# Holding back the first four output stores of a sparse convolution and issuing them from ScalarE's queue

## The chip, the cores and the metric

One core of one Trainium2 chip. The metric is device time of one execution in microseconds (us). The profile's span (first to last instruction) is about 2 us shorter. A transfer is "issued" when an engine's queue starts it and "landed" when its last byte is reported written. In the profile lines PE is TensorE, DVE VectorE, ACT ScalarE, POOL GpSimd and SP SyncE; a q behind the name (ACTq) is that engine's instruction queue, and PEclk is the clock granted to TensorE in tenths of full speed. A run on one core is called slow when it is over 1.5% above the fastest of the same kernel; fast runs alone enter the ratios.

## The reference

A 3x3 convolution, padding 1, 16 images of 64 channels of 64x64, 128 output channels. The weights are 90% zeros, but scattered, so the kernel treats them as dense.

```python
batch, c_in, h, w, c_out, k = 16, 64, 64, 64, 128, 3
x_pad = np.pad(x, ((0, 0), (0, 0), (pad, pad), (pad, pad)), mode='constant')
output[b, co] += weight[co, ci, kh, kw] * x_pad[b, ci, kh:kh+h, kw:kw+w]   # for all b, co, ci, kh, kw
```

In bytes: 16.8 MB of input and 33.6 MB of output, both fp32.

## The kernel before

Two images (64 channels each) stand one above the other on 128 partitions, so the work is eight pairs. All input loads but the first half pair (fp32, on SyncE's queue) are queued at the start on GpSimd's queue and cast to bf16 on the way. Each pair has four blocks of 16 rows. A block, but for the very first, is three products on TensorE (a shared one, even rows, odd rows); ScalarE copies the shared product to SBUF and VectorE adds it to the other two, into an output tile of 2 MB per image. Seven such tiles are taken in turn; the first also serves as landing place of the first half pair of input.

```python
o_pool = ctx.enter_context(tc.tile_pool(name="o", bufs=7))
psum_pool = ctx.enter_context(
    tc.tile_pool(name="psum", bufs=8, space=bass.MemoryType.PSUM)
)
# ...
x_head = o_pool.tile([128, H, W], FP32, name="o")
# ...
for p in range(1, NP):
    nc.gpsimd.dma_start(out=xs[p], in_=pair(p))
# ...
    shared = product([(s, G1, 0, 1)], 8)              # in twos(): one block
    for n in range(2):
        c = p_pool.tile([128, 8, W], FP32, name="pc")
        nc.scalar.copy(out=c, in_=shared[n])          # L161
    # ...
            nc.vector.tensor_tensor(                  # L168
                out=o[n][:, first : r0 + 16 : 2, :], in0=ps[n], in1=pc[n], op=ADD
            )
# ...
for p in range(NP):
    o = [o_pool.tile([C_OUT, H, W], FP32, name="o") for _ in range(2)]
    # ... four blocks; the last pair is stored in halves
    if not last:
        for n in range(2):
            nc.sync.dma_start(out=out[2 * p + n], in_=o[n])
```

Of the kernel before, what the change touches and what calls it, by code (L numbers as in the profile page):

```python
# [27 lines left out]
def kernel(  # L28
# [6 lines left out]
    nc = tc.nc  # L35

    B, C_IN, H, W = x.shape
# [106 lines left out]
    def direct(p, o, r0, rows):  # L144
        ps = product(
            [(xs[p], G1, r0, 1), (xs[p], G0, r0 - 1, 1), (xs[p], G2, r0 + 1, 1)], rows
        )
        nc.scalar.copy(out=o[0][:, r0 : r0 + rows, :], in_=ps[0])  # L148
        nc.vector.tensor_copy(out=o[1][:, r0 : r0 + rows, :], in_=ps[1])  # L149

    def twos(p, o, r0):
        t0 = r0 // 2
        s = s_pool.tile([128, 8, W], BF16, name="s")
        nc.gpsimd.tensor_tensor(  # L154
            out=s, in0=xs[p][:, r0 : r0 + 16 : 2, :], in1=xs[p][:, r0 + 1 : r0 + 16 : 2, :], op=ADD
        )
        shared = product([(s, G1, 0, 1)], 8)
        pc = []
# [3 lines that stand above are left out]
            pc.append(c)  # L162
        even = [(xs[p], G21, r0 + 1, 2), (xs[p], G0, r0 - 1, 2)]
        odd = [(xs[p], G01, r0, 2), (xs[p], G2, r0 + 2, 2)]
        for first, terms in ((r0, even), (r0 + 1, odd)):
            ps = product(terms, 8)
            for n in range(2):
                nc.vector.tensor_tensor(  # L168
                    out=o[n][:, first : r0 + 16 : 2, :], in0=ps[n], in1=pc[n], op=ADD
                )  # L170

    for p in range(NP):
        o = [o_pool.tile([C_OUT, H, W], FP32, name="o") for _ in range(2)]
        last = p == NP - 1
        for blk in range(4):
            r0 = 16 * blk
            if BLOCKS[p][blk] == "T":
                twos(p, o, r0)
            else:
                for r, rows in ((r0, 8), (r0 + 8, 8)):  # L180
                    direct(p, o, r, rows)
            if last and blk % 2 == 1:
                for n in range(2):
                    rows = slice(r0 - 16, r0 + 16)
                    nc.sync.dma_start(out=out[2 * p + n][:, rows, :], in_=o[n][:, rows, :])
        if not last:
            for n in range(2):
                nc.sync.dma_start(out=out[2 * p + n], in_=o[n])


# [28 lines left out]
```

## Time and profile before

| | before |
|---|---|
| time, median (first 3 runs) | 127.66 us (127.59 to 127.90) |
| span of the profile | 125.4 us |
| TensorE's products | 7.1 to 109.2 us without a gap |
| last two stores issued, landed | 111.2 and 111.8, 121.8 and 124.2 us |
| DMA | full from about 1.8 to 122 us |

The strips cut the span in 40 slices of 3.1 us; a digit is the busy share in tenths. The lines themselves, and how they are read, stand in the prediction below.

### The profile page before, as it was taken

The page shows a single profiled execution, that of the slowest core. Times are in us where ns is not written, and L with a number is a line of the kernel's source. Part 1 is how long each engine was busy: PE and PEld are TensorE (multiplying, and loading weights), DVE is VectorE, ACT ScalarE, POOL GpSimd, SP SyncE. Part 2 cuts the span into 40 slices and gives each one's busy share as a digit, 9 for nine tenths or more (in the row PEclk, how much of TensorE's full clock was granted, in tenths as well). Part 3 has the DMA queues.
Part 4 walks back from the last instruction along what each step waited for, and adds up shares of the span by engine and source line. Part 5 has one row for each costly group of instructions (what it writes and reads, how often), then busy time and mean ns, then how long its engine had stood idle before and what let it go on. Part 6 is the DMA issues. An engine that isn't in the chain of part 4 may idle for free.

```text
span 125.4 us, 2486 instructions
## 1 busy us (share of the span) xinstructions
PE 107.5 (86%) x1002; PEld 58.8 (47%) x1002; DVE 82.4 (66%) x135; ACT 39.0 (31%) x71; POOL 40.7 (32%) x45
## 2 busy tenths in 40 slices
PE   6679999999999999999999999999999999920000
PEld 6435555555555555555555555555555555500000
DVE  0463877877787778777877787778777877760000
ACT  4555323333333333333333333333333333300000
POOL 6936533333333333333333333333333300000000
PEclk9999999999999999999999999999999999997555
DMA  5999999989999999999999999999999999999980
GB/s 146 338 222 220 212 214 220 191 259 350 324 311 337 308 293 319 342 316 308 426 429 423 408 429 434 450 416 434 418 418 429 429 444 423 434 397 423 423 369 10
DMA packets 4044, 42.93 MB, mean 342 GB/s; under 512 B 448, under 2 KB 448, under 8 KB 704
## 3 DMA queue, kind: packets, MB, share of 16 engines
q1 hardware_dynamic: 2880, 34.90, 66.2%
q0 software_dynamic: 1152, 7.86, 30.7%
q8 instruction: 8, 0.13, 0.4%
q14 instruction: 4, 0.03, 0.1%
HBM read 17.07 MB, written 33.55 MB: 404 GB/s over the span
## 4 chain that ended last, share of the span: by engine, by line
PE 81%; DMA 4%; DVE 1%; issue 1%; DVEq 0%; SPq 0%
PE ps L135 81%; DMA o<-in_x_dram 4%; DVE o L168 1%; DVEq L214 0%; DVE x L87 0%; SPq L60 0%; DVEq L168 0%
## 5 line engine op out<-in xcount | busy, mean ns | idle before, releaser
L168 DVE TENSOR_TENSOR o<-ps,pc 128x512 f32<-128x512 f32 x124 | 77.8, 686 | 22.1 <-PE ps L135 19.8
L135 PE MATMUL ps<-x,wT 64*128 64x504 bf16 (+3 forms) x780 | 88.8, 373 | 1.5 <-DVE x L87 1.5
L135 PEld LDWEIGHTS <-wT 64*128 64x128 bf16 x966 | 55.2, 94 | 49.4 <-issue 1.5
L154 POOL TENSOR_TENSOR s<-x 128x512 bf16<-128x512 bf16 x31 | 35.6, 1152 | 57.7 <-PE ps L135 41.5
L161 ACT COPY pc<-ps 128x512 f32<-128x512 f32 x62 | 33.3, 589 | 64.0 <-issue 61.8
L135 PE MATMUL ps<-s,wT 64*128 64x512 bf16 (+1 forms) x186 | 25.7, 377 | 0.0
L74 PE MATMUL ps<-idle_rhs 128*128 128x128 bf16 x27 | 3.1, 310 | 1.0 <-DVE idle_rhs L71 1.0
L67 POOL DMA_DIRECT2D x<-in_x_dram x7 | 3.7, 561 | 0.0
L74 PEld LDWEIGHTS <-idle_rhs 128*128 128x128 bf16 x27 | 2.8, 144 | 1.0 <-DVE idle_rhs L71 1.0
L91 DVE CAST w_bf<-w_sb 128x192 bf16<-128x192 f32 (+1 forms) x4 | 1.3, 382 | 3.0 <-DMA w_sb<-in_weight_dram 3.0
L149 DVE COPY o<-ps 128x512 f32<-128x512 f32 x2 | 1.4, 692 | 2.0 <-PE ps L135 2.0
L148 ACT COPY o<-ps 128x512 f32<-128x512 f32 x2 | 1.2, 586 | 2.4 <-PE ps L135 2.4
L87 ACT CAST x<-o 128x576 bf16<-128x576 f32 (+1 forms) x2 | 1.5, 802 | 0.5 <-DMA o<-in_x_dram 0.5
L91 ACT ACT_TABLE_LOAD x1 | 1.3, 1283 | 0.7 <-PEq L203 0.7
L97 PE MATMUL ps<-ident,w_bf 128*128 128x128 bf16 x9 | 1.1, 292 | 0.4 <-DVE w_bf L91 0.4
L87 DVE CAST x<-o 128x576 bf16<-128x576 f32 x1 | 0.5, 460 | 1.4 <-DMA o<-in_x_dram 1.4
L91 ACT CAST w_bf<-w_sb 128x64 bf16<-128x64 f32 (+1 forms) x2 | 0.7, 418 | 1.9 <-DMA w_sb<-in_weight_dram 1.9
L97 PEld LDWEIGHTS <-w_bf 128*128 128x128 bf16 x9 | 0.8, 128 | 0.8 <-DVE w_bf L91 0.8
L101 DVE TENSOR_TENSOR wT<-ps,wT 128x384 bf16<-128x384 f32 x2 | 1.0, 550 | 0.0
L63 POOL DMA_DIRECT2D x<-in_x_dram x1 | 0.7, 696 | 0.8 <-POOLq L203 0.8
L71 DVE MEMSET idle_rhs<- 128x64 uint32 x1 | 0.1, 112 | 0.8 <-PEq L203 0.8
L110 ACT CAST wT<-ps 128x384 bf16<-128x384 f32 x1 | 0.5, 481 | 0.4 <-PE ps L97 0.4
(8 smaller groups left out, 1.9 us busy)
## 6 DMA issues: line engine op xcount, KB each, us to landing
out_dram<-o SPq DMA_DIRECT2D x14, 2048.0 KB, 19.8
x<-in_x_dram POOLq DMA_DIRECT2D x7, 1024.0 KB, 29.3
out_dram<-o SPq DMA_DIRECT2D x4, 1024.0 KB, 12.3
o<-in_x_dram SPq DMA_DIRECT2D x1, 1024.0 KB, 5.4
x<-in_x_dram POOLq DMA_DIRECT2D x1, 512.0 KB, 7.5
w_sb<-in_weight_dram SPq DMA_DIRECT2D x1, 288.0 KB, 3.1
```

The source lines that it names most:

```text
L67: nc.gpsimd.dma_start(out=xs[p], in_=pair(p))
L74: nc.tensor.matmul(idle_ps, idle_rhs, idle_rhs, start=True, stop=True)
L87: copy(out=xs[0][:, a:b, :], in_=x_head[:, a:b, :])
L91: copy(out=w_bf4[:, g, a:b, :], in_=w_v[:, k : k + b - a, :])
L97: nc.tensor.matmul(wps[:, j, :], src, ident, start=True, stop=True)
L101: nc.vector.tensor_tensor(out=wT[:, g], in0=wps, in1=wT[:, G1], op=SUB)
L135: nc.tensor.matmul(ps[n][:, lo:hi, c_lo:c_hi], tap(g, kw, n), src[q, a:b:step, c_lo + kw - 1 : c_hi + kw - 1], start=(i == 0), stop=(i == ...
L148: nc.scalar.copy(out=o[0][:, r0 : r0 + rows, :], in_=ps[0])
L149: nc.vector.tensor_copy(out=o[1][:, r0 : r0 + rows, :], in_=ps[1])
L154: nc.gpsimd.tensor_tensor(out=s, in0=xs[p][:, r0 : r0 + 16 : 2, :], in1=xs[p][:, r0 + 1 : r0 + 16 : 2, :], op=ADD)
L161: nc.scalar.copy(out=c, in_=shared[n])
L168: nc.vector.tensor_tensor(out=o[n][:, first : r0 + 16 : 2, :], in0=ps[n], in1=pc[n], op=ADD)
```

## The change

The intent: as long as loads run, no stores; the first two pairs' outputs stay in their tiles and go out once the loads are about through. ScalarE's queue issues them, because SyncE's queue would otherwise have to wait in the middle of its order.

```diff
+    HELD = 2
+    held = []
+
+    def store(engine, p, n, o, a, b):
+        engine.dma_start(out=out[2 * p + n][:, a:b, :], in_=o[n][:, a:b, :])
+
 ... (four blocks of a pair) ...
             if last and blk % 2 == 1:
                 for n in range(2):
-                    rows = slice(r0 - 16, r0 + 16)
-                    nc.sync.dma_start(out=out[2 * p + n][:, rows, :], in_=o[n][:, rows, :])
-        if not last:
+                    store(nc.sync, p, n, o, r0 - 16, r0 + 16)
+            if p == HELD and blk == 1:
+                for args in held:
+                    store(nc.scalar, *args)
+        if p < HELD:
+            held += [(p, n, o, 0, H) for n in range(2)]
+        elif not last:
             for n in range(2):
-                nc.sync.dma_start(out=out[2 * p + n], in_=o[n])
+                store(nc.sync, p, n, o, 0, H)
```

## The prediction

> **What bounds the kernel now.** I read the page from the bottom limit upwards: first the strips by slice (is any engine, or the DMA, full from end to end?), then the chain of work that ended last, then the DMA queues stretch by stretch, and last the waits of the queue that issues the stores.
>
> The page's strips and totals first. The span is 125.4 us, so a slice is 3.135 us.
>
> ```profile
> PE   6679999999999999999999999999999999920000
> DVE  0463877877787778777877787778777877760000
> DMA  5999999989999999999999999999999999999980
> GB/s 146 338 222 220 212 214 220 191 259 350 324 311 337 308 293 319 342 316 308 426 429 423 408 429 434 450 416 434 418 418 429 429 444 423 434 397 423 423 369 10
> ```
>
> Two things are full: TensorE from slice 3 to slice 34, and the DMA engines from slice 1 to slice 38. TensorE ends at about 110 us; the DMA engines go on for four more slices. The end of the kernel is therefore set by bytes still to be stored. The GB/s row shows three stages under one and the same DMA strip of nines: about 217 GB/s (loads alone), about 320 (loads and stores mixed), about 427 (stores alone, from slice 19).
>
> The chain, merged, in order of time, and then the waits of the store-issuing queue:
>
> ```profile
> 7.12 102.09 PE ps L135 x954
> ...
> 109.88 0.68 DVE o L168
> 110.56 0.60 DVEq L214
> 111.16 0.60 DVE o L168
> ```
>
> ```profile
> SPq L188 <- DVE o L168: 92.2, 14, 19.9
> SPq L214 <- DMA out_dram<-o: 11.6, 4, 4.4
> ```
>
> The chain follows TensorE to 109.2 us and VectorE to 111.8 us, and stops there because it ends with the last instruction of a compute engine. The second fence has the rest: at its end SyncE waited 11.6 us in total for the last four stores to land. Read alone, the chain would send one after TensorE; but the last two stores (1 MB each, 2.1 MB together, 4.9 us at 427 GB/s) are issued at 111.2 and 111.8 and land at 121.8 and 124.2 (10.6 and 12.4 us from issue to landing), so some 6 us of older stores still stood before them in the queue. TensorE has about 5 us of slack; the DMA has none.
>
> The DMA queues, in three stretches: 7 to 21 us, 35 to 48 us, 74 to 100 us. Columns are packets, MB, and the share of the 16 engines' time.
>
> ```profile
> q0 software_dynamic: 443, 3.04, 104.2%
> ```
>
> ```profile
> q0 software_dynamic: 195, 1.47, 54.0%
> q1 hardware_dynamic: 191, 2.64, 48.5%
> ```
>
> ```profile
> q1 hardware_dynamic: 759, 11.13, 100.6%
> ```
>
> q0 holds the casting loads, q1 the stores. Alone, loads bring 3.04 MB in 14 us = 217 GB/s (as bf16; twice that is read). Stores alone write 11.13 MB in 26 us = 428 GB/s. Now the question that decides this change: does mixing them cost anything? In 35 to 48 us, 1.47 MB of loads would take 6.8 us alone, 2.64 MB of stores 6.2 us; together 13.0 us, and the stretch is 13 us. Mixing costs nothing there. In 22 to 35 us the trace has 1.54 MB of loads (7.1 us) and 2.08 MB of stores (4.9 us), 12.0 of 13 us; some 0.6 us of the missing 1 us lies between 24 and 26 us, where the first stores enter and only 0.32 MB moves although the engines count as busy. So the whole price of mixing before is about 1 us, and most of it is a price of starting, not of mixing.
>
> **What the Trainium skill says.** "DMA: Bandwidth & Descriptors", section "Issuing engines are not separate DMA queues": transfers started by ScalarE, SyncE or GpSimd run on the same 16 engines and interleave. The trace agrees as far as it can: the shares of q0 and q1 add up to about 100% in every stretch. The same page, "Queues, rings and completion order": each DMA engine goes round-robin between the queue rows that have work, a packet at a time. The trace agrees: 195 against 191 packets in the mixed stretch. From this I take that ScalarE's and SyncE's queues, both with 16 KB rows to store, will share half and half. "Latency and other measured facts" gives some 0.6 us to the first byte for this kind of queue; the trace differs: the first stores are issued at 21.6 us, and between 24 and 26 us only three of their packets run, so behind a full load queue it is about 4 us.
>
> **The change part by part.**
>
> Instructions: no TensorE, VectorE or GpSimd instruction is added, removed or moved. ScalarE gets four DMA issues after its 18th copy of L161, which is the one ending at 38.5 us (third pair, second block). On SyncE's queue such an issue takes 0.33 us, so four are about 1.4 us; ScalarE idles 2.2 us there before its next copy at 40.7. Cost on the path: 0. Their data have been complete since 34.9 us, when the second pair's stores were issued before, so they wait for nothing.
>
> Removed: stores of 8.4 MB between 21.6 and 38.5 us. The loads get the engines alone: 7.86 MB in all less 3.36 MB moved by 21 us leaves 4.5 MB, at 217 GB/s 20.7 us, so the loads end at about 42 us (from landings of the fourth load at 24.1 us and 4.9 us apiece, 43.6) instead of 62.8 us. No one needs them earlier: no wait on a load is longer than 2.2 us before, and that one is at 13.8 us. Gain on the path: 0.
>
> Moved: the held stores start at 38.5 + 4 = about 42.5 us, just as the loads end. A gap of 0 to 0.8 us, or an overlap.
>
> Sum for the DMA, from 24.1 us on. Before: 4 loads at 4.9 us and the equal of 16 full stores at 5.0 us (landings from 64.2 to 124.2 are twelve full-size equivalents in 60.0 us) = 99.6, so 123.7, against 124.2 seen. After: the same sum, 123.7, with the start-up loss either there or not: 123.7 to 124.5. The end moves by -0.5 to +0.3 us. The work is only reordered, and the engines were full.
>
> Output buffers: there are seven, taken in turn, the first by the loaded head. So the fourth pair's second image reuses the first held buffer, the fifth pair both of the next two, the sixth pair's first image the last. With landings at half rate after SyncE's queue joins (third pair's stores issued at 47.2, moving at about 51):
>
> First held store: 42.5 + 5.0 + rest of the loads = about 48.5. VectorE wants that buffer at 48.9 (its four adds start at 48.3, the second 0.6 later). No wait, or up to 1 us.
>
> Second: by 51 us 1.6 stores are done; the remaining 0.4 at half rate take 4 us, so 55. Wanted at 61.1. No wait.
>
> Third: 10 us more, 65 to 66.5. Wanted at 61.7. VectorE waits 3.5 to 4.7 us. This is the new wait. TensorE has eight banks in use as four pairs of products, and may run on until it needs the banks of the product three before, about 1.9 us; so TensorE stalls 1.5 to 3 us.
>
> Fourth: 10 us more, 75 to 76.5. Wanted at 73.9 plus the stall, 76. Wait 0 to 1 us, taken up by the same 1.9 us.
>
> TensorE then ends at 111 to 113 instead of 109.2, and the last two stores are issued by about 115. To end at 123.7 they have to be in the queue by 123.7 - 4.9 - 0.5 = about 118. They are. Cost on the path: 0. Predicted sum: -0.3 us, so 127.66 becomes 127.4.
>
> **The rivals.** First, mixing reads and writes really costs the memory something and separate stages are faster. For it: the 1 us missing between 22 and 35 us, and the author's intent. Against: the 35 to 48 us stretch balances to 0.1 us. It would give at most 1 us: 126.6.
>
> Second, the buffer wait becomes the bound: if SyncE's queue gets two thirds instead of half, the third held store lands near 73 us, VectorE waits 11 us, TensorE ends near 119 and the last stores come too late for a full DMA; about 129 to 131. For it: the wait is real under any sharing, and the deeper stores all stand behind it. Against: equal packets, and the even 195 to 191.
>
> Third, ScalarE's queue drains wholly before SyncE's (descriptors made in order of issue). Then the third store lands at 58.5, no wait at all, and the time is 127.4 as well. The total does not tell this from my story; the wait at the fifth pair does.
>
> Fourth, the queue of ScalarE starts late or the loads end early, and the engines stand still for 1 to 3 us near 42 us. Each idle microsecond goes to the end: up to 130.
>
> **Range and chances.** The centre is 127.4. Downward there is only the 1 us of mixing loss: 126.5. Upward there are a gap of some tenths and part of the second and fourth rivals: 129.0. Faster by over 2% would be below 125.1, which needs 2.5 us of DMA work to vanish: 3%. Slower by over 2% is above 130.2: 8%. Within: 89%.
>
> **What would show it.** In the changed profile the GB/s strip should read about 217 until slice 12 or 13 and then about 427 to the end, with the DMA strip still all nines; the last load should land at 42 to 44 us. The waits of VectorE should have a new row, L168 waiting for a store, 3 to 5 us at about 62 us and little elsewhere, and TensorE a stall of 1.5 to 3 us soon after it. The final wait of SyncE should shrink by as much as TensorE ends later. I am wrong if the DMA strip shows a hole near 42 us, if the stores-only rate differs from 427 GB/s with two store queues at work, or if the last stores land at once after their issue, which would mean that compute has become the bound.

## More of the kernel before

The profile of the kernel before is of a run of 127.12 us, which is not among the timed ones and is faster than all of them. It also has the earliest start of the fourteen profiles: TensorE's first 36 products on image data took 3.99 us in it, 5.35 to 6.92 us in the others.

## The result, and the profile after

| | before | after |
|---|---|---|
| time, median | 127.71 us (4 runs) | 127.67 us (4 runs) |
| ratio of fast runs | | 0.9996 (0.9978 to 1.0014) |
| the same, five more rounds | | 1.0003 (0.9987 to 1.0019) |
| profiled run, span | 125.4 us | 126.0 us |

A ratio is the mean time of one kernel's fast runs over that of the other's fast runs of the same rounds, so not quite the ratio of the medians. The time did not change.

The strips of the changed kernel (slices of 3.15 us):

```profile
PE   6569999999999999999994999999999999992000
PEclk9968999999999999999999999999999999999555
DMA  4999999999999999999999999999999969999990
GB/s 133 349 229 213 213 211 213 224 219 213 211 211 219 330 421 437 416 421 424 447 432 421 432 406 437 442 432 414 427 421 447 401 250 421 458 401 406 419 385 26
```

The three stages have become two: about 215 GB/s to slice 12, about 425 from slice 14. The mixed stage is gone, and nothing was won by it: the DMA strip is as full as before and ends in the same slice. Two new dents: a 4 in TensorE at slice 21, and a 6 in the DMA at slice 32 (100.8 to 104 us). The GB/s of the slice is 250 there. Counted from the packets' times in the trace, not all engines paused in that dent: all 16 were busy until 100.5 us, three still at 102.75, and all again at 103.0.

The chain, merged, and the waits (who, for whom: us in total, times, longest):

```profile
40.20 26.77 DMA out_dram<-o
...
67.09 0.70 DVE o L168
67.80 0.04 issue
67.84 44.88 PE ps L135 x406
...
113.42 1.28 DVE o L168 x2
114.69 0.60 DVEq L226
```

```profile
DVE o L168 <- DMA out_dram<-o: 3.5, 1, 3.5
...
PE ps L135 <- DVE o L168: 1.6, 1, 1.6
```

```profile
SPq L226 <- DMA out_dram<-o: 8.1, 4, 2.4
```

The chain of before ran through TensorE alone; now a store stands in it: issued at 40.2 us, landed at 67.0, and VectorE waited 3.5 us for its tile. TensorE then stood for 1.6 us. SyncE's last wait shrank from 11.6 to 8.1 us, by as much as VectorE's end moved (from 111.8 to 115.3). So compute came later and the end did not.

How ScalarE's and SyncE's queues share, between 55 and 67 us (packets, MB, share of 16 engines); q10 is ScalarE's:

```profile
q1 hardware_dynamic: 176, 2.62, 51.2%
q10 hardware_dynamic: 171, 2.51, 49.2%
```

Half and half. And ScalarE at the place of the four issues:

```profile
39.31 0.38 ACTq L178 DMA_DIRECT2D out_dram<-o  x1
39.68 0.59 ACT L161 COPY pc<-ps 128x512 f32<-128x512 f32 x1
39.72 3.55 ACTq L178 DMA_DIRECT2D out_dram<-o  x3
43.39 1.07 ACT L161 COPY pc<-ps 128x512 f32<-128x512 f32 x2 [3.12 <-DVE o L168]
```

The four issues took until 43.27 us, not the 1.4 us of the prediction; the fourth alone took 2.31 us, and the next copies came 1 us late (43.39 in place of 42.4, one block of 3.2 us after those at 39.2). The releaser in brackets is a case of the rule that a wait is put down to the last semaphore: what really held ScalarE was its own queue.

TensorE's end moved by 3.5 us, but only half of that is the change. In this run the granted clock was low early (PEclk 6 in slice 2), and the first shared-product copy of ScalarE came at 13.5 us in place of 11.8. From the first such copy to the last it is 97.9 us after and 96.2 before: 1.8 us belong to the change. The Trainium skill, "TensorE: Matmul & The Clock Gate", Part 1, says that the activity window which raises the clock runs freely, so that the number of slow products at the start differs from run to run. The runs here agree that the start varies: the first 36 products took 5.60 us here and 6.80 us in the repeat below, and the first copy came between 11.8 and 15.3 us, in kernels whose start is the same. That the clock alone is the reason is not shown: in the repeat PEclk reads 9 throughout the start.

### The profile page after: what moved, and what is told of

Its sections match the earlier page's. It is cut to its first block, busy times and chain, and to the rows that moved or that the text cites. A ratio compares the mean times of both kernels' runs of the same rounds, so it can differ in the third digit from the quotient of the medians.

```text
span 126.0 us, 2485 instructions
## 1 busy us (share of the span) xinstructions
PE 109.1 (87%) x1002; PEld 58.1 (46%) x1002; DVE 82.0 (65%) x135; ACT 39.0 (31%) x71; POOL 40.7 (32%) x45
## 4 chain that ended last, share of the span: by engine, by line
PE 59%; DMA 26%; issue 2%; DVE 2%; DVEq 1%; ACT 0%; SPq 0%; ACTq 0%
PE ps L135 59%; DMA out_dram<-o 21%; DMA o<-in_x_dram 4%; DVE o L168 2%; DVEq L226 0%; ACT pc L161 0%; DVE x L87 0%; SPq L60 0%; ACTq L178 0%; DVEq L168 0%
## 5 line engine op out<-in xcount | busy, mean ns | idle before, releaser
L135 PE MATMUL ps<-x,wT 64*128 64x504 bf16 (+3 forms) x780 | 93.2, 378 | 3.8 <-DVE x L87 2.2
L161 ACT COPY pc<-ps 128x512 f32<-128x512 f32 x62 | 33.3, 589 | 65.8 <-issue 54.3
L135 PE MATMUL ps<-s,wT 64*128 64x512 bf16 (+1 forms) x186 | 28.1, 377 | 0.0
L112 DVE CAST wT<-ps 128x384 bf16<-128x384 f32 x1 | 0.6, 550 | 0.0
```

What stands on the lines that cost most here:

```text
L135: nc.tensor.matmul(ps[n][:, lo:hi, c_lo:c_hi], tap(g, kw, n), src[q, a:b:step, c_lo + kw - 1 : c_hi + kw - 1], start=(i == 0), stop=(i == ...
```

## The experiments

In the table, "first" and "last" are the starts of ScalarE's first and last shared-product copies (L161), "seventh" is the issue of the seventh pair's first store on SyncE, "landed" the last landing; all are from the profiles, in us. The last column is the landing less the seventh pair's issue. "Slow runs in it" are slow by the 1.5% rule alone: their granted clock is that of the fast runs (0.957 to 0.958 against 0.959 to 0.969 for eight tiles, 0.953 to 0.954 against 0.948 to 0.953 for late), and what makes them longer is not shown.

| kernel | first | last | seventh | landed | difference | median time |
|---|---|---|---|---|---|---|
| before | 11.78 | 107.95 | 98.38 | 124.20 | 25.8 | 127.7 |
| after | 13.54 | 111.48 | 101.91 | 124.81 | 22.9 | 127.67 |
| after, again | 14.92 | 111.19 | 101.62 | 124.53 | 22.9 | 127.75 |
| one queue | 13.54 | 109.72 | 100.15 | 124.81 | 24.7 | 127.74 |
| eight tiles | 14.91 | 115.31 | 105.74 | 128.65 | 22.9 | 130.15 (slow runs in it) |
| issues parted | 13.60 | 111.45 | 101.88 | 124.85 | 23.0 | 127.52 |
| late | 13.44 | 110.12 | 100.55 | 128.61 | 28.1 | 134.48 (slow runs in it) |
| reversed, by name | 14.80 | 111.48 | 101.91 | 124.81 | 22.9 | 127.65 |
| reversed, fixed tiles | 13.83 | 133.99 | 124.42 | 147.34 | 22.9 | 149.47 |

### The changed kernel again

No edit. 

> The changed kernel again, for a second profile and a tighter interval. My theory (the DMA engines are full from 2 us on and only the order of their work changed): ratio to the kernel before 0.995 to 1.005; VectorE waits 3 to 4.5 us for the third held store and TensorE stalls 1 to 3 us after it. The 1.7 us by which TensorE was behind before the third pair in the first profile should not be part of the change: it goes with a lower granted clock in the first 10 us and should be absent when the clock is 9 or 10 tenths there. Rival (unmixed stages save 1 us, the stall gives it back): same ratio here; the next two runs tell.

Measured: ratio 1.0003 (0.9987 to 1.0019). The profile was another one: VectorE waited for no store at all. TensorE began later, the third pair's stores were issued at 50.9 us in place of 48.9, ScalarE's queue had the DMA longer to itself, and the third held store landed at 62.3 us in place of 67.0, before it was wanted. ScalarE lost more instead:

```profile
41.11 4.76 ACTq L178 DMA_DIRECT2D out_dram<-o  x3
45.99 2.14 ACT L161 COPY pc<-ps 128x512 f32<-128x512 f32 x4 [4.34 <-PE ps L135]
```

Three issues took 4.76 us and four copies then ran in one go, but from the first to the last copy this run took 96.3 us, 0.1 more than before. So the wait of 3.5 us that I had foreseen is not a fixed property of the change: it depends on how early compute starts. The expectation of a wait in each run missed. My idea that the late start should be absent where the strip shows full clock missed too: PEclk reads 9 in every early slice here and the first copy came at 14.9 us.

### All stores on one queue

```diff
             if p == HELD and blk == 1:
+                store(nc.sync, p, 0, o, 0, 16)
                 for args in held:
-                    store(nc.scalar, *args)
+                    store(nc.sync, *args)
...
-                store(nc.sync, p, n, o, 0, H)
+                store(nc.sync, p, n, o, 16 if p == HELD and n == 0 else 0, H)
```

> The same hold, but all stores go out on SyncE's queue in order (a first quarter of the third pair's first image goes ahead of the held ones, so that SyncE waits until then). ScalarE issues nothing. My theory: the third held store lands near 59 us, no wait of VectorE for a store over 1 us, TensorE ends 1.5 to 2 us earlier than in the changed kernel at the same clock, SyncE's last wait grows by as much, and the time stays: ratio to before 0.995 to 1.005. Rival (unmixed stages save 1 us and the stall of TensorE gave it back): 126.7 us, ratio 0.99 to 0.994.

Measured: ratio 1.0000 (0.9984 to 1.0015). The third held store landed at 60.7 us. The wait line, and the strips:

```profile
DVE o L168 <- DMA out_dram<-o: 0.4, 1, 0.4
```

```profile
DMA  4999999999999999999999999999999999999950
GB/s 132 348 225 211 213 221 216 216 216 208 219 219 221 302 427 427 437 416 427 424 428 436 432 422 432 432 427 414 432 432 427 406 427 432 432 390 419 432 247 13
```

The stall is gone (96.2 us between the copies, as before), the hole at 100 us is gone, TensorE ends 1.8 us earlier than in the first profile of the changed kernel at the same start, and the time is the same: the last store lands at 124.81 us in both. The hole has moved to the end: slice 38 is a 5 here and a 9 there. Most of the 16 DMA engines are through earlier, and the last landing waits for one that is not: counted from the packets' times, one engine alone is at work from 122.75 to 124.3 us here, and from 122.5 to 123.7 us in the kernel before. The slow issues came along to SyncE's queue: the four held stores took 0.43, 0.47, 2.44 and 1.57 us to issue, so they do not belong to ScalarE. This speaks against the rival by which unmixed stages save 1 us that the stall gives back: without the stall, the saving should appear, and the interval leaves no room for more than 0.2 us of it.

### Eight output tiles

Eight tiles do not fit (the program does not build: 128 KB per partition wanted, 124.8 left), so the last pair's input reuses the first pair's tile.

```diff
-    o_pool = ctx.enter_context(tc.tile_pool(name="o", bufs=7))
+    o_pool = ctx.enter_context(tc.tile_pool(name="o", bufs=8))
...
+        if p == 0:
+            xs.append(x_pool.tile([128, H, W], BF16, name="x0"))
+            nc.gpsimd.dma_start(out=xs[7], in_=pair(7))
```

> The changed kernel with eight output buffers in place of seven; the space comes from the last pair's load reusing the first pair's input tile, so it is issued at about 21 us, long before the load queue is through. My theory: the fifth pair now waits for the first two held stores, which land at 50 and 57 us, so there is no wait at 62 us; the sixth pair's second image waits 0 to 3 us for the fourth held store (77 us); TensorE loses under 1 us; time as before, ratio 0.995 to 1.005. Rival (stall gave back a gain): ratio 0.99 to 0.994.

Measured: ratio of fast runs 1.0056 (1.0013 to 1.0098); three of six runs were slow, and the profile is of a slow one. It is no clean test: I replaced one wait by another. GpSimd's queue, in order, waited for the first pair to be through before it could issue the load and go on to the second pair's sums.

```profile
PE ps L135 <- POOL s L154: 2.4, 1, 2.4
```

```profile
PE   6669999399999999999999999999999999992000
DMA  4999999999999099999999999999999969999990
```

TensorE lost some 4 us at 24 us (two blocks took 6.1 and 4.4 us in place of 3.2), so ScalarE issued the held stores at 44.9 us, after the last load had landed at 43.6, and the DMA stood empty for a slice. Inconclusive for its question, and a warning for the experiments' design.

### The issues on ScalarE parted

```diff
-            if p == HELD and blk == 1:
-                for args in held:
+            if p == HELD and blk in (1, 2):
+                for args in held[2 * blk - 2 : 2 * blk]:
```

> The changed kernel with the four issues on ScalarE's queue parted: two after the third pair's second block, two after its third. In the changed kernel the fourth issue took 2.31 us and held the next copies back by 1 us. If an issue is slow because more than three 2 MB stores stand in the queue before the first has begun, the four here take 0.3 to 0.8 us each and no copy of ScalarE is late. If the slow issue is due to the load queue being full, they stay slow. The time is the same under both, 0.995 to 1.005.

Measured: ratio 0.9986 (0.9968 to 1.0004); issues of 0.37, 0.46, 0.34 and 1.32 us, and no copy late (42.50, 45.74). So parting does away with the delay of the copies, and one issue still takes over a microsecond, against the 0.3 to 0.8 us expected. VectorE waited 3.4 us for the third held store as in the first profile. As an explanation this is half: in the repeat of the changed kernel the second issue already took 2.2 us, with one store ahead of it. What an issue waits for is left open.

### Fewer bytes, before and after

Both kernels with only 48 of 64 rows stored in pairs four to seven, wrong results: 4.2 MB less, 9.8 us at 428 GB/s.

```diff
-                nc.sync.dma_start(out=out[2 * p + n], in_=o[n])
+                rows = slice(0, 48 if 3 <= p <= 6 else H)
+                nc.sync.dma_start(out=out[2 * p + n][:, rows, :], in_=o[n][:, rows, :])
```

```diff
-                store(nc.sync, p, n, o, 0, H)
+                store(nc.sync, p, n, o, 0, 48 if 3 <= p <= 6 else H)
```

> The kernel before, with only 48 of 64 rows of the outputs of pairs four to seven stored (wrong results on purpose): 4.2 MB or 9.8 us of DMA work less, computing the same. Theory that the DMA end sets the time: until now some 6 us of older stores stood before the last two; they are gone, so the end becomes the last issue at 111.8 us plus about 1 us plus 4.9 us for the two last stores, near 118 us: 6 us faster, 121.5 us, ratio 0.945 to 0.965. Rival that TensorE's chain sets the end now: under 1 us faster, ratio over 0.99.

> The changed kernel with the same rows left out (wrong results on purpose). The first three pairs' stores are untouched, so VectorE's wait of 3 to 4.5 us and TensorE's stall of about 1.6 us stay. With the DMA no longer full, the stall should show: 1.5 to 3 us slower than the kernel before with the same rows left out (123 to 124.5 us, ratio to the kernel before 0.96 to 0.98). If the stall is made up anyway, the two are equal within 0.5 us.

Measured: 122.75 us and 124.12 us, ratios 0.9626 (0.9544 to 0.9707) and 0.9700 (0.9630 to 0.9770), which overlap. So both again with five rounds:

> The kernel before with 48 of 64 rows stored in pairs four to seven, again (wrong results on purpose), for the comparison with the next run on the same chip: 122.3 to 123.3 us.

> The changed kernel with the same rows left out, again. In the first pair of such runs the medians were 1.4 us apart, but the profile of this one showed no wait of VectorE for a store, and TensorE had begun 1.9 us later. If the buffer wait costs when the DMA is not full: 0.5 to 2 us over the run before this one, with the interval of the two ratios apart; and between the first and the last shared-term copy of ScalarE 96.5 us or more against 96.2. If the 1.4 us were the start alone, the two ratios overlap within 0.3%.

Measured: 122.85 and 123.81 us, ratios 0.9595 (0.9550 to 0.9639) and 0.9705 (0.9667 to 0.9743), apart. (The kernel before came out 1.2 us above the centre of its expectation, within the ratio that it named; that the wait of VectorE would stay in the changed kernel missed, as told below.) The DMA strips of the repeat, first the kernel before, then the changed one:

```profile
DMA  4999999999999999999999999999999469749693
```

```profile
DMA  4999999999999999999999999999997069849593
```

With 9.8 us of stores taken away and every computation left in, the kernel before is about 5 us faster, and the DMA is no longer full in the last quarter. That is the proof that the DMA set the end before: TensorE's chain alone could not have given 5 us. The other 5 us are not had, because compute then sets the end.

And once compute sets the end, the change costs: 1.4 us by the difference of the second pair of ratios (0.0110 of 127.7). That ratio leaves out two of the six runs of the kernel before as slow; with all six the means are 122.8 and 123.8 us, 1.0 us apart, and in the first pair 123.0 and 124.1. So about 1 us is the safer figure, and that the intervals are apart rests on the two runs left out. Where the 1 us comes from is settled only in part. The profiles of the changed kernel with fewer rows show no wait of VectorE for a store, and between first and last copy 96.5 us against 96.2, so 0.3 us; the rest of the distance in these two profiles is a later start (15.0 against 13.8). What fits all profiles is this: in every kernel with the held stores on ScalarE from the third pair's second block on and an otherwise untouched compute (six profiles, the two with fewer rows among them; not "late", where it is 110.12) the last copy stands at 111.2 to 111.9 us, whether the first came at 13.5 or at 15.3; where nothing is held on ScalarE it is the first plus 96.2 us (from 107.95 upwards). A late start is hardly delayed further (0.1 to 0.5 us), an early one is delayed by the buffer wait (1.7 to 1.8 us). That is an inference; no run sets the start.

### The hold ends later

```diff
-            if p == HELD and blk == 1:
+            if p == HELD and blk == 3:
```

> The held stores go out after the third pair's last block, about 6.3 us later (near 45.5 us on ScalarE), when the loads have been through since 42 to 43 us. The theory: the DMA engines stand empty for 3 to 4 us, and that goes to the end, because they are full after it: 130.5 to 132 us, ratio 1.02 to 1.035. VectorE waits at the fourth pair too (first held store lands at about 51.5 us against 48.9 wanted). Rival: a hole is made up because the DMA has slack; then the ratio is within 1.005.

Measured: the two fast runs 131.62 and 132.85 us, ratio 1.0335 (1.0229 to 1.0440); two more were slow and are left out. The profile is of the first of these.

```profile
DMA  4999999999999079999999999999999999999970
```

The last load landed at 43.8 us, ScalarE issued at 45.7, the first store packet ran at 46.6: the DMA stood for 3 us (the 0 and the 7). The last store landed at 128.61 us, 3.8 later than in the changed kernel, while ScalarE's last copy (110.12 us) was 1.4 us earlier. VectorE waited twice, 1.6 and 2.9 us. So an empty DMA goes to the end in full, and a wait of compute does not.

### The held stores in reversed order

```diff
-                for args in held:
+                for args in held[::-1]:
```

> The held stores in reversed order, so that the buffer wanted first (at 49 us by the fourth pair) is stored last. The theory: the first pair's first image lands near 72 us in place of 50, VectorE stands for 20 to 23 us, TensorE for about 20, the DMA engines run dry from 72 to 85 us, and the time is 136 to 142 us. A small cost (under 132 us) would say that the order in the queue does not matter.

Measured: 127.65 us, ratio 0.9976 (0.9888 to 1.0065), far from the 136 to 142 expected. The built program tells why: the tile pool hands out the tile whose release comes first, so the fourth pair got the tile that was now stored first. Nothing was reversed but the names. With seven tiles taken in fixed turn, and the order reversed as above:

```diff
+    o_bufs = [o_pool.tile([128, H, W], FP32, name=f"o{i}") for i in range(7)]
...
-        o = [o_pool.tile([C_OUT, H, W], FP32, name="o") for _ in range(2)]
+        o = [o_bufs[(1 + 2 * p + n) % 7] for n in range(2)]
```

> The reversed order once more, now with the seven output buffers as named tiles taken in fixed turn (in the run before, the pool handed the fourth pair the buffer that was stored first, so nothing was reversed but the names). The built program now makes the fourth pair's second image wait for the store issued last. The theory: that store lands near 72 us and is wanted near 50, so VectorE waits 20 to 24 us, TensorE stands about 20 us, the DMA runs dry for 10 us and more before 85 us, and the time is 139 to 146 us. Under 132 us would say that the order in the queue does not matter.

Measured: 149.47 us, ratio 1.1717 (1.1656 to 1.1779).

```profile
DVE o L169 <- DMA out_dram<-o: 23.3, 1, 23.3
PE ps L136 <- DVE o L169: 21.4, 1, 21.4
```

```profile
DMA  5999999999999999999300069919958983999991
GB/s 172 290 226 216 212 214 216 223 212 216 214 320 422 433 433 430 433 437 441 128 4 0 0 282 424 419 79 424 437 205 353 424 353 146 424 422 399 417 417 46
```

VectorE waited 23.3 us for the store that landed last, at 74.3 us, as the theory said; TensorE stood 21.4 us. The time is above my range because I counted 20 us for TensorE and some slack on top. There was none: the last copy is 22.5 us later than in the changed kernel (133.99 against 111.48), and the last landing is too (147.34 against 124.81). So a wait of the same kind that cost nothing at 3.5 us costs its full length beyond the slack.

### A try at a faster kernel

The kernel before, with one of the last stores cut so that one DMA engine should carry none of its first part. The Trainium skill, "DMA: Bandwidth & Descriptors", section "Why a DMA increments its semaphore by 16 and not by 1", says that a transfer uses the largest number of engines up to 16 that divides its outer dimension, and that a store from SyncE's queue then uses the lowest-numbered ones; so 120 partitions use 15, and not the last. No run here shows which engine carries what.

```diff
-                    nc.sync.dma_start(out=out[2 * p + n][:, rows, :], in_=o[n][:, rows, :])
+                    parts = (slice(0, 120), slice(120, 128)) if blk == 1 and n == 1 else (slice(0, 128),)
+                    for q in parts:
+                        nc.sync.dma_start(out=out[2 * p + n][q, rows, :], in_=o[n][q, rows, :])
```

> A try at a faster kernel: the kernel before, with the store of the last pair's second image, first half, cut into partitions 0 to 119 and 120 to 127, so that the last of the 16 DMA engines carries nothing of the first part. At the end of every profile most engines are through 2 us before the last landing. If the last engine is the straggler, 0.5 to 1 us faster: ratio 0.992 to 0.996. If another engine is the straggler, 0.998 to 1.003.

Measured: 129.36 us, ratio 1.0123 (1.0098 to 1.0148): slower than either guess. The strips:

```profile
DMA  4999999999999999999999999999999999999981
GB/s 131 345 224 213 213 223 213 215 164 300 325 338 302 323 328 313 336 320 415 438 436 420 425 430 441 415 430 433 430 420 430 379 420 430 446 366 282 282 377 54
```

In slices 36 and 37, where the cut store runs, the engines count as busy but move 282 GB/s in place of 420. The uneven cut makes packets slower: those of 8 KB took 0.31 us each in the kernel before, and 0.33 to 0.67 us on average in each microsecond of that stretch; why, no run tells. No version here beats the two kernels.

## Why the prediction was right or wrong

**The bound.** Right. Fewer stored bytes made the kernel 4% faster with the same compute; an empty DMA of 3 us made it 3.8 us later at the last landing; a delay of compute of 1.8 us, present or absent, changed nothing.

**Mixing costs nothing.** Right. The changed kernel has no mixed stage, and the version without the stall has neither mixed stage nor stall; both are within 0.2% of before. The predicted gain of 0.3 us was not seen; the intervals of five rounds leave room for 0.2 us. The time in which engines count as busy did fall a little: the queues' shares add up to 97.4% of 125.4 us before and 96.7% of 126.0 after, 122.1 and 121.8 us. The step "stores of 8.4 MB between 21.6 and 38.5 us" is a misreading, as those are the times of issue and the four stores landed from 37.2 to 64.2 us; no sum uses it.

**Where the moved stores land.** Near: predicted about 48.5, 55, 65 to 66.5 and 75 to 76.5 us, seen 50.0, 57.3, 67.0 and 76.8. The half-and-half sharing was right. The time to the first packet was 2.9 us (issued at 39.3, first packet at 42.2) where I took 4. The last load landed at 46.4 in place of 42 to 44; at 43.8 in the repeat.

**The new wait.** Right in the first profile (3.5 us for VectorE, 1.6 for TensorE; predicted 3.5 to 4.7, where its own landings give 3.3 to 4.8, and 1.5 to 3), absent in the second. The close agreement is in part luck: the tile was wanted at 63.5 us and the store landed at 67.0, both later than predicted. So is that of TensorE's end, 112.7 us for 111 to 113, as half of its shift is the late start. The step that was too simple is "Wanted at 61.7": that time moves with the start of compute by up to 3 us, and so does SyncE's queue joining in.

**ScalarE's issues.** The term was mis-sized: 4 issues at 0.33 us make 1.4 us, measured 3.96 and 5.2 us. I took the duration from a queue in which no issue had to wait. It cost nothing because the copies caught up in the next block.

**The slack of compute.** The step that failed quietly is "To end at 123.7 they have to be in the queue by 123.7 - 4.9 - 0.5 = about 118". It looked at the last two stores alone. The tight place lies earlier: from the seventh pair's first store on, 8.4 MB are still to go, 19.6 us at 428 GB/s, and the profiles show 22.9 us from that issue to the last landing wherever compute is the later of the two (last column of the table, six profiles from 101.6 to 124.4 us). Before, that store was issued at 98.4 and 25.8 us passed, so the slack was 25.8 - 22.9 = 2.9 us, not 5, and that in a profile with an early start. In the first profile after, the store came 3.5 us later and all of the slack was used: that is the hole at slice 32. The rival that the wait becomes the bound was therefore nearer than the 8% I gave to slower suggests: another 3 us of delay would have cost 2%. That the hole did not show in the time fits the packets: three engines never paused in it, and from 122.75 us to the last landing only one to four are still at work. The version on one queue has no hole and lands at the same 124.81 us. But in the changed kernel the end already follows compute: in the repeat that issue came 0.29 us earlier and the last landing 0.28. So the two limits met within a few tenths, and that the time did not change at all is in part luck.

## What to carry to other kernels

When one resource is full from end to end, reordering its work gains only what the order itself costs, whatever the strips look like (here nothing that could be measured); work that out first from the profile's own rates. Then size the slack of everything else from the place where it is smallest, here the seventh pair's first store, not from the last instruction, and allow for a start that varies by 3 us from run to run. A held store holds its tile: look up who wants that tile next, and when, and remember that a tile pool may hand out another one when the order of releases changes.

## What the Trainium skill lacked or had wrong

- "DMA: Bandwidth & Descriptors", "Latency and other measured facts": about 0.6 us to the first byte. Here 0.9 us on an idle DMA (issued 45.7, first packet 46.6), and behind a full load queue 1.4 and 2.9 us in the two profiles of the changed kernel and 4.2 us in the kernel before.
- No page that I found: how the cost of an issue grows when large stores are already queued. Here 0.3 to 2.5 us for one of 2 MB on ScalarE's queue, with ScalarE's copies waiting behind it (1.0 and 2.2 us late in the two profiles of the changed kernel), and up to 2.4 us on SyncE's.
- "DMA: Bandwidth & Descriptors", the same section, says that DMA engines 7 and 15 are usually slower. The profiles agree that the engines drift apart (in the version on one queue one engine works alone for the last 1.5 us), but the trace does not name them. With fewer rows, where the DMA had paused before the last two stores, all 16 ended within about 0.5 us of each other, so the lag seen here is one of a long full stretch.
- No page that I found: the rate of a store cut at 120 of 128 partitions. Here 282 GB/s in place of 420 with the two parts in the queue, the engines counted as busy, and 1.2% on the time.
